# A fourth seven-product chunk pair in every second gate-and-up block of a two-FFN decoder layer

## The chip, the cores and the metric

The kernel runs on one NeuronCore of a Trainium2 chip. The metric is the device time of one execution in microseconds, as the median over several executions. The profiled execution is one more execution of the same program; its span is what the trace covers.

## The reference

The reference is one decoder layer over 256 tokens of width 2048, in float32. Four parts follow each other:

```python
x = x + 0.5 * swiglu(rms_norm(x, ffn1_norm), ffn1_w_gate, ffn1_w_up, ffn1_w_down)
x = gated_parallel_mixer(x, ...)      # sliding-window attention and RWKV-7, gated
x = memory_cross_attention(x, mem, ...)
x = x + 0.5 * swiglu(rms_norm(x, ffn2_norm), ffn2_w_gate, ffn2_w_up, ffn2_w_down)
return rms_norm(x, final_norm)

def swiglu(h, w_gate, w_up, w_down):
    return (silu(h @ w_gate) * (h @ w_up)) @ w_down
```

The hidden width of each feed-forward network is 5632. Only the two feed-forward networks and the place where the mixer's constants are made are touched by the change.

## The kernel before, in words

**Products.** TensorE multiplies in a reduced float32 format, so each operand is split into a high part (a cast on ScalarE, `hi`) and the rest (a subtraction on VectorE, `lo`). One product of a 128x128 block of the activations with a 128x512 piece of weights is three matmuls, L422 (high by high), L423 (high by the weights' low part) and L424 (low by high), in the function `times`. Weights come from memory as float32 (`raw`, `raw2`), are split by `split_raw` (L330 cast, L331 subtraction), and are used by both halves of 128 tokens.

**Blocks.** A feed-forward network has 11 blocks of 512 hidden columns, in groups of 4, 4 and 3 (`GROUPS`). Block 0 multiplies gate and up one after the other (`product`). In blocks 1 to 10 `gate_up` does both in one `product_pair`. Its contraction over 2048 runs in eight chunk pairs q = 0 to 7 of 256 each. After each group come the down products for that group (`down`, also through `product_pair`, or `product`).

**Seven products for eight.** A plain chunk pair takes two halves of tokens times gate and up times two chunks, that is eight products or 24 matmuls. In the chunk pairs of `SEVEN = (0, 2, 4)` a Strassen-like scheme takes seven products, named p1 to p7, or 21 matmuls. It needs four sums of weight pieces t1 to t4, built by `sums` for each chunk pair: L350, L351 and L352 on VectorE, then the cast L355 on ScalarE and the subtraction L356 on VectorE (tiles `thi` and `tlo`, one buffer each). It also needs sums of the activations, built once for each network by `combinations` (L454 to L470; tiles `chi`, `clo`). A plain chunk pair that comes before the last seven-product one (`EARLY`, here 1 and 3) needs another, smaller sum of the activations for p3. Products are added over all eight chunk pairs in PSUM. After the last seven-product pair, `end` (L559 to L561) adds the shared terms, and after q = 7 `finish` (L565 to L577) makes silu(gate) times up.

**Buffers.** `raw2` has 3 buffers, each holding one chunk pair of gate and up. The weights' `hi` and `lo` have 3 buffers each; a seven-product pair fills two of them (`u1g1`, 1024 columns, and `g0`, 512 columns) beside `thi` and `tlo`, and a plain pair fills two of 1024 columns. PSUM has four single banks (`acc`) and two double banks (`two`); p6 and p7 share one double bank, p5 and p3 the other, and the transposes of the block's result (`feats`) use the same two.

**Order.** The program is traced in Python. `next_item` asks for the splits of the present and of the next chunk pair (`AHEAD`), and `Interleave.tick` puts steps of background work between the products: the transposes, the combinations, the norms. A scheduler of the language then fixes the order of each engine's instructions when the program is built, and may place an instruction that its model finds ready ahead of earlier ones. At run time each engine goes through its own fixed list.

**Constants.** Masks and small matrices for the mixer are made at the program's start on GpSimd (L213 to L244) in a pool that lives through the whole kernel.

Of the kernel before, what the change touches and what calls it, by code (L numbers as in the profile page):

```python
# [15 lines left out]
P = 128  # L16
# [24 lines left out]
EARLY = tuple(q for q in range(max(SEVEN)) if q not in SEVEN)  # L41

SEVEN_DOWN = (2, 4)
# [46 lines left out]
def feed_forward_plan(wg, wu, wd):  # L90
    for gi, (j0, nj) in enumerate(GROUPS):
        for j in range(j0, j0 + nj):
            if j == 0:
                for w in (wg, wu):
                    yield w, 0, KD, j * 512, 512
            else:
                yield (wg, wu), 0, KD, (j * 512, j * 512), SEVEN
        for n in (0, 2):
            if n in down_pairs(gi):
                yield (wd, wd), 4 * j0, 4 * nj, (n * 512, n * 512 + 512), SEVEN_DOWN  # L100
            else:
                for m in (n, n + 1):
                    yield wd, 4 * j0, 4 * nj, m * 512, 512
# [37 lines left out]
def decoder_layer(ctx: ExitStack, tc: tile.TileContext, a: dict, out: bass.AP):  # L141
# [71 lines left out]
    identr = cpool.tile([P, P], F32R, name="identr")  # L213
    select(identr[:], ones[:], [[-1, P]], ALU.is_equal, 0.0, 0, 1)
    abias = cpool.tile([P, 2, P], F32R, name="abias")
    pool.memset(f32(abias[:]), 0.0)
    select(abias[:, 0, :], abias[:, 0, :], [[1, P]], ALU.is_gt, NEG, 0, -1)
    select(abias[:, 1, :], abias[:, 1, :], [[-1, P]], ALU.is_ge, NEG, 0, 1)

    ups = cpool.tile([P, P], F32, name="ups")  # L220
    pool.memset(ups[:], UP)
    mask3 = cpool.tile([P, 3, P], F32, name="mask3")
    select(mask3[:, 0, :], ups[:], [[1, P]], ALU.is_gt, 0.0, 0, -1)
    select(mask3[:, 1, :], ups[:], [[1, P]], ALU.is_ge, 0.0, 0, -1)
    select(mask3[:, 2, :], ups[:], [[1, P]], ALU.is_ge, 0.0, 0, -1)

    mask_l = cpool.tile([P, P], F32, name="mask_l")
    select(mask_l[:], ups[:], [[-1, P]], ALU.is_gt, 0.0, 0, 1)
    bdones = cpool.tile([P, P], F32, name="bdones")
    bdmean = cpool.tile([P, P], F32, name="bdmean")  # L230
    bdup = cpool.tile([P, P], F32, name="bdup")
    pool.memset(bdones[:], 0.0)
    pool.memset(bdmean[:], 0.0)
    pool.memset(bdup[:], 0.0)
    for e in range(2):
        q = slice(64 * e, 64 * e + 64)
        pool.memset(bdones[q, q], 1.0)
        pool.memset(bdmean[q, q], 1.0 / 64)
        pool.memset(bdup[q, q], UP)
    center = cpool.tile([P, P], F32, name="center")  # L240
    dve.tensor_tensor(center[:], ident[:], bdmean[:], ALU.subtract)
    keep = cpool.tile([P, 2, P], F32, name="keep")
    pool.memset(keep[:], 1.0)
    pool.memset(keep[:, :, 0:1], 0.0)  # L244
# [189 lines left out]
    def combinations(sp, x, seven, early, ready, tag, apart):  # L434


        n = 4 * len(seven) + 2 * len(early)
        parts = [sp.tile([P, n, P], F32R, tag=tag + e, name=tag + e) for e in ("hi", "lo")]
        c = {"parts": parts, "at": {}, "next": []}

        def work():
            o = 0
            while not ready():
                yield
            yield from idle(apart)
            for q in sorted(seven + early):
                while not all(KU * q + i in x.done for i in range(KU)):
                    yield
                v = sp.tile([P, 2, 2, P], F32, tag="u", name="u", bufs=2)
                f = sp.tile([P, 4, P], F32, tag="u", name="u", bufs=2)  # L450
                n = 4 if q in seven else 2
                s = slice(o, o + n)
                with behind_weights():
                    dve.tensor_tensor(  # L454
                        v[:].rearrange("p k t n -> p k (t n)"), f32(x.at(0, 2 * q, 2)),
                        f32(x.at(1, 2 * q, 2)), ALU.add,
                    )
                    if q in seven:
                        dve.tensor_tensor(f[:, 0], v[:, 0, 1], v[:, 1, 1], ALU.add)
                        dve.tensor_tensor(f[:, 1], f[:, 0], v[:, 0, 0], ALU.subtract)  # L460
                        dve.tensor_tensor(f[:, 2], v[:, 0, 0], v[:, 0, 1], ALU.subtract)
                        dve.tensor_tensor(f[:, 3], v[:, 1, 0], f[:, 1], ALU.subtract)
                    else:
                        dve.tensor_tensor(f[:, :2], v[:, :, 0], v[:, :, 1], ALU.subtract)
                yield from idle(2)
                with behind_weights():
                    act.copy(parts[0][:, s], f[:, :n])
                yield from idle(2)
                with behind_weights():
                    dve.tensor_tensor(  # L470
                        parts[1][:, s], f[:, :n], f32(parts[0][:, s]), ALU.subtract
                    )
                c["at"][q] = o
                o += n
                yield

        bg.spawn("mem", work())
        return c

    def product_pair(x: Act, c, w, four, seven, early, after, end, finish, first=()):  # L480
# [10 lines left out]
        def bank(to):  # L491
            if to in b:
                return
            for pair in PAIRS:
                if to in pair:
                    banks = two()
                    b.update((e, banks[:, i]) for i, e in enumerate(pair))
                    return
            b[to] = acc()
# [12 lines left out]
        def of_c(q, i):  # L512
            return [p[:, c["at"][q] + i, :] for p in c["parts"]]

        p5 = "p8" if four else "p5"
        for q in range(late + 1):
# [3 lines left out]
            if q in seven:  # L520
# [16 lines left out]
                continue  # L537
            u = next_item()
            for i in range(KU):
                for to, t, j in (("p2", 0, 0), ("p4", 1, 0), ("p3", 0, 1), (p5, 1, 1)):  # L540
                    off = to == "p3" and q in early
                    ends = last and i == KU - 1
                    add(to, of_c(q, i) if off else of_x(t, k + i), u[i][j], ends)
# [5 lines left out]
    PAIRS = ("p6", "p7"), ("p5", "p3")  # L549

    def gate_up(sp, x, c, r, w):
        hb = sp.tile([P, 2, 512], F32, tag="hb", name="hb", bufs=2)
        u2, u3 = (sp.tile([P, 512], F32, tag="u", name="u", bufs=2) for _ in range(2))
# [4 lines left out]
        def end(b):  # L558
            dve.tensor_tensor(u2[:], b["p6"], hb[:, 0], ALU.add)  # L559
            dve.tensor_tensor(u3[:], b["p7"], u2[:], ALU.add)  # L560
            dve.tensor_tensor(u2[:], b["p5"], u2[:], ALU.add)  # L561
            while c["next"]:
                bg.spawn("feat", c["next"].pop())

        def finish(to, b):  # L565
# [3 lines left out]
            elif to == "p4":  # L569
                dve.tensor_tensor(hb[:, 1], b["p4"], u3[:], ALU.add)  # L570
                act.activation(hb[:, 1], hb[:, 1], AF.Silu, scale=r[1])
            else:
                t, v = (0, u2) if to == "p3" else (1, u3)
                dve.tensor_tensor(v[:], b[to], v[:], ALU.add)  # L574
                dve.scalar_tensor_tensor(
                    hb[:, t], v[:], r[t], hb[:, t], ALU.mult, ALU.mult
                )  # L577

        product_pair(x, c, w, False, SEVEN, EARLY, after, end, finish)
        return hb  # L580

    def down(sp, h, c, w, xs, then):
# [17 lines left out]

        def residual():
# [3 lines left out]
            for t, v in enumerate((hb, u)):  # L605
                yield
                o = xs(t, 0, 2)
                dve.tensor_tensor(o, v[:].rearrange("p a n -> p (a n)"), o, ALU.add)
# [10 lines left out]
        product_pair(  # L619
            h, c, w, True, SEVEN_DOWN, (), after, end, finish,  # L620
            ("p1", "p5"),
        )
# [99 lines left out]
    def feed_forward(sp, x, norm: Norm, wg, wu, wd, done, begin_last=lambda: None, last=False):  # L722
# [7 lines left out]
        c = combinations(sp, norm.x, SEVEN, EARLY, lambda: norm.r is not None, "c", 4)  # L730
        for gi, (j0, nj) in enumerate(GROUPS):
# [9 lines left out]
            for j in range(j0, j0 + nj):  # L741
                if j > 0:
                    hb = gate_up(sp, norm.x, c, norm.r, wg)
# [11 lines left out]
                for t in range(2):  # L755
                    dve.scalar_tensor_tensor(
                        hb[:, t, :], pu[t], norm.r[t], hb[:, t, :], ALU.mult, ALU.mult
                    )
# [4 lines left out]
            d = combinations(sp, h, SEVEN_DOWN, (), lambda: True, "d", 0)  # L763
            for n in (0, 2):
                if n in down_pairs(gi):
                    down(
                        sp, h, d, wd,
# [4 lines left out]
                for m in (n, n + 1):  # L772
# [3 lines left out]
                    for t in range(2):  # L776
                        xs = x[:, t, m * 512 : (m + 1) * 512]
                        dve.scalar_tensor_tensor(xs, pd[t], 0.5, xs, ALU.mult, ALU.add)
# [70 lines left out]
    with tc.tile_pool(name="mx", bufs=1, reuse_waits="tile") as sp:  # L849
        aligned(sp)  # L850

# [885 lines left out]
```

## Time and profile before

| | |
|---|---|
| median of 3 executions | 2235.72 us (2234.56 to 2239.03) |
| profiled execution | 2236.75 us, span 2235.0 us |
| granted TensorE clock in the profile | 0.999 |
| TensorE matmul busy | 2216.0 us, 99% of the span, 10792 matmuls |
| VectorE busy | 1745.4 us, 78%, 2039 instructions |
| ScalarE busy | 1193.5 us, 53% |
| DMA | 435.40 MB, mean 195 GB/s |

A row of the timeline has the start in us from the span's start, the duration, the engine, the line of the kernel, the operation, output and inputs, their shapes, how many instructions were merged into the row, and in brackets how long the engine was idle before and which instruction ended that. Matmuls overlap, so the time that one costs is the distance between two starts and not its duration. VectorE's instructions overlap a little as well, so the distance of starts is used for them too.

Block j = 1 of the first network runs from about 55 to 97 us, block 2 to about 141 us, block 3 to about 184 us; then follow the down products of the first group. The mixer begins at about 720 us, the second network's block 0 at about 1524 us.

### The profile page before, as it was taken

To read this page: it belongs to the slowest core of one execution; us is meant where nothing else is said; L and a number is where in the kernel's file an instruction comes from. 1 tells how busy PE (TensorE), PEld (TensorE's weight loads), DVE (VectorE), ACT (ScalarE), POOL (GpSimd) and SP (SyncE) were. 2 spreads that over 40 slices of the span, in tenths; PEclk is the share of its full clock that TensorE was granted. 3 is DMA by queue.
4 is the path that set the end of the run, shared out by engine and by line. 5 is a ranking of instruction groups with operands and counts; after the bars stand their busy time and mean duration, and the time that the engine had idled before them with its cause. 6 is when DMAs were issued, how large, how long until landed. Compare 5 with 4: busy or idle time off the path is not lost.

```text
span 2235.0 us, 28341 instructions
## 1 busy us (share of the span) xinstructions
PE 2216.0 (99%) x10792; PEld 1819.2 (81%) x10792; DVE 1745.4 (78%) x2039; ACT 1193.5 (53%) x1434; POOL 81.3 (4%) x151
## 2 busy tenths in 40 slices
PE   9999999999999999999999999999999999999998
PEld 7888888888888877788888878888888888888886
DVE  7988988898987567886465466558888888898887
ACT  6555555555555567444443445556555555555554
POOL 1000000000000000103200100001000000000000
PEclk9999999999999999999999999999999999999999
DMA  7666665566556545677435775547665656566664
GB/s 247 211 220 195 203 207 190 187 208 202 194 193 214 165 130 151 219 219 233 121 102 148 230 266 189 181 164 255 201 207 177 218 193 199 193 202 194 207 203 155
DMA packets 219832, 435.40 MB, mean 195 GB/s; under 512 B 13888, under 2 KB 16016, under 8 KB 219696
## 3 DMA queue, kind: packets, MB, share of 16 engines
q1 hardware_dynamic: 210768, 406.37, 56.8%
q0 software_dynamic: 8352, 26.44, 3.8%
q8 instruction: 84, 1.38, 0.3%
q10 hardware_dynamic: 576, 0.79, 0.1%
q14 instruction: 52, 0.43, 0.1%
HBM read 420.05 MB, written 13.50 MB: 194 GB/s over the span
## 4 chain that ended last, share of the span: by engine, by line
PE 93%; DVE 3%; DMA 2%; ACT 1%; issue 1%; SPq 0%; POOLq 0%; POOL 0%; DVEq 0%; ACTq 0%
PE acc L422 20%; PE acc L423 20%; PE acc L424 20%; PE two L422 9%; PE two L423 9%; PE two L424 9%; PE two L185 2%; DVE lo L331 1%; PE two L177 1%; DMA raw<-in_ffn_w_up_dram 1%; DMA raw<-in_w_proj_rwkv_dram 1%; ACT hi L330 0%; PE two L1279 0%; DMA raw<-in_ffn_w_gate_dram 0%; PE acc L1416 0%
## 5 line engine op out<-in xcount | busy, mean ns | idle before, releaser
L330 ACT CAST hi<-raw 128x1024 fp32r<-128x1024 f32 (+1 forms) x770 | 764.2, 1001 | 783.7 <-PE acc L424 362.1
L331 DVE TENSOR_TENSOR lo<-raw,hi 128x1024 fp32r<-128x1024 f32 (+1 forms) x770 | 882.5, 1156 | 343.0 <-ACT hi L330 342.2
L422 PE MATMUL acc<-hi,xhi 128*128 128x512 f32 (+1 forms) x1256 | 491.2, 392 | 1.9 <-ACT hi L330 1.8
L423 PE MATMUL acc<-lo,xhi 128*128 128x512 f32 (+1 forms) x1256 | 488.2, 389 | 2.8 <-DVE lo L331 2.8
L424 PE MATMUL acc<-hi,xlo 128*128 128x512 f32 (+1 forms) x1256 | 486.9, 388 | 0.0
L422 PEld LDWEIGHTS acc<-hi,xhi 128*128 128x128 f32 x1256 | 235.7, 188 | 56.0 <-issue 5.4
L423 PEld LDWEIGHTS acc<-lo,xhi 128*128 128x128 f32 x1256 | 235.9, 188 | 55.2 <-DVE lo L331 6.7
L424 PEld LDWEIGHTS acc<-hi,xlo 128*128 128x128 f32 x1256 | 235.8, 188 | 47.4 <-DVE xlo L680 0.2
L356 DVE TENSOR_TENSOR tlo<-raw,thi 128x1024 fp32r<-128x1024 f32 x160 | 192.8, 1218 | 0.0
L355 ACT CAST thi<-raw 128x1024 fp32r<-128x1024 f32 x160 | 165.7, 1050 | 36.6 <-DVE raw L350 20.1
L423 PE MATMUL acc<-lo,hhi 128*128 128x512 f32 x424 | 166.4, 392 | 0.0
L424 PE MATMUL acc<-hi,hlo 128*128 128x512 f32 x424 | 165.2, 390 | 0.0
L422 PE MATMUL acc<-hi,hhi 128*128 128x512 f32 x424 | 159.8, 391 | 0.0
L422 PE MATMUL two<-hi,xhi 128*128 128x512 f32 x320 | 125.7, 393 | 0.0
L424 PE MATMUL two<-hi,xlo 128*128 128x512 f32 x320 | 124.6, 389 | 0.0
L423 PE MATMUL two<-lo,xhi 128*128 128x512 f32 x320 | 124.6, 389 | 0.0
L350 DVE TENSOR_TENSOR raw<-raw 128x1024 f32<-128x1024 f32 x80 | 97.5, 1219 | 15.4 <-DMA raw<-in_ffn_w_up_dram 13.1
L423 PEld LDWEIGHTS acc<-lo,hhi 128*128 128x128 f32 x424 | 79.6, 188 | 19.4 <-DVE lo L331 3.1
L422 PEld LDWEIGHTS acc<-hi,hhi 128*128 128x128 f32 x424 | 79.1, 188 | 18.6 <-ACT hi L330 2.6
L424 PEld LDWEIGHTS acc<-hi,hlo 128*128 128x128 f32 x424 | 79.6, 188 | 16.2
L422 PEld LDWEIGHTS two<-hi,xhi 128*128 128x128 f32 x320 | 60.1, 188 | 13.4 <-DVE u L574 0.2
L424 PEld LDWEIGHTS two<-hi,xlo 128*128 128x128 f32 x320 | 60.1, 188 | 12.6
(374 smaller groups left out, 3186.2 us busy)
## 6 DMA issues: line engine op xcount, KB each, us to landing
raw<-in_ffn_w_gate_dram SPq DMA_DIRECT2D x167, 512.0 KB, 3.8
raw<-in_ffn_w_up_dram SPq DMA_DIRECT2D x160, 512.0 KB, 4.7
raw<-in_ffn_w_down_dram SPq DMA_DIRECT2D x152, 512.0 KB, 4.8
raw<-in_w_in_dram SPq DMA_DIRECT2D x136, 512.0 KB, 3.7
raw<-in_w_out_dram SPq DMA_DIRECT2D x32, 512.0 KB, 3.6
raw<-in_ffn_w_down_dram SPq DMA_DIRECT2D x12, 1024.0 KB, 5.2
raw<-in_ffn_w_up_dram SPq DMA_DIRECT2D x8, 1024.0 KB, 7.9
raw<-in_w_proj_attn_dram SPq DMA_DIRECT2D x16, 512.0 KB, 4.2
```

The lines of the kernel that those rows point to most:

```text
L177: prev = pe.matmul(to, lhs, rhs, **how)
L185: prev = pe.transpose(to, src, ident[:])
L330: newest["act"] = act.copy(hi[:, s], raw[:, s])
L331: newest["dve"] = dve.tensor_tensor(lo[:, s], raw[:, s], f32(hi[:, s]), ALU.subtract)
L350: dve.tensor_tensor(ta[:], raw[:, 1:3], raw[:, 0:2], ALU.subtract)
L355: act.copy(hi[:, s], t[:])
L356: dve.tensor_tensor(lo[:, s], t[:], f32(hi[:, s]), ALU.subtract)
L422: pe.matmul(o, xh, hi, start=first, stop=False, **how)
L423: pe.matmul(o, xh, lo, start=False, stop=False, **how)
L424: newest["pe"] = pe.matmul(o, xl, hi, start=False, stop=last, **how)
```

## The change

- In odd blocks (1, 3, 5, 7, 9 of each network) `gate_up` takes seven products in chunk pairs 0, 2, 3 and 4 (`MORE`); even blocks keep 0, 2 and 4. Chunk pairs 2, 3 and 4 of an odd block are then three seven-product pairs in a row, and the weight plan follows.
- `combinations` builds the activation sums for 0, 2, 3 and 4, and the smaller ones for 1 and 3, so that chunk pair 3 has both kinds (6 sets where there were 5). Its work tile becomes one buffer of [128, 2, 512] in place of two of 512 columns.
- The last steps of both token halves become one: p3 and p5 are added to their shared terms in one instruction of 1024 columns after p5, and multiplied with the silu in a second one. The norm's factor is no longer multiplied in here.
- That factor, times 0.5, is applied where the down products are added to the residual stream. Block 0 and `down` change with it.
- The mixer's constants are made at the start of the mixer, in its own pool, in place of the program's start.

```diff
+MORE = (0, 2, 3, 4)
 SEVEN_DOWN = (2, 4)
+def early(*sets):
+    return tuple(sorted({q for s in sets for q in range(max(s)) if q not in s}))
+def seven_up(j):
+    return MORE if j % 2 else SEVEN
...
-                yield (wg, wu), 0, KD, (j * 512, j * 512), SEVEN
+                yield (wg, wu), 0, KD, (j * 512, j * 512), seven_up(j)
...
-    identr = cpool.tile([P, P], F32R, name="identr")
...
+    def mixer_constants(sp):
+        identr = sp.tile([P, P], F32R, name="identr")
...
-            for q in sorted(seven + early):
+            for q in sorted(set(seven + minus)):
...
-                v = sp.tile([P, 2, 2, P], F32, tag="u", name="u", bufs=2)
-                f = sp.tile([P, 4, P], F32, tag="u", name="u", bufs=2)
+                w = sp.tile([P, 2, 512], F32, tag="u", name="u", bufs=1)
...
+                todo = []
+                if q in seven:
+                    todo.append(4)
+                if q in minus:
+                    todo.append(2)
...
-    PAIRS = ("p6", "p7"), ("p5", "p3")
+    PAIRS = ("p6", "p7"), ("p3", "p5")
...
-            else:
-                t, v = (0, u2) if to == "p3" else (1, u3)
-                dve.tensor_tensor(v[:], b[to], v[:], ALU.add)
-                dve.scalar_tensor_tensor(
-                    hb[:, t], v[:], r[t], hb[:, t], ALU.mult, ALU.mult
-                )
-
-        product_pair(x, c, w, False, SEVEN, EARLY, after, end, finish)
+            elif to == "p5":
+                dve.tensor_tensor(u[:], b["p3", "p5"][:], u[:], ALU.add)
+                dve.tensor_tensor(hb[:], u[:], hb[:], ALU.mult)
+
+        product_pair(x, c, w, False, seven, early(seven), after, end, finish)
...
-        def half(o, of, in1):
-            dve.scalar_tensor_tensor(o, of, 0.5, in1, ALU.mult, ALU.add)
-
         def after(b):
-            act.activation(hb[:, 0], b["p1"], AF.Copy, scale=0.5)
+            act.copy(hb[:, 0], b["p1"])
 
         def end(b):
-            half(hb[:, 1], b["p6"], hb[:, 0])
-            half(u[:, 0], b["p7"], hb[:, 1])
-            half(hb[:, 1], b["p5"], hb[:, 1])
-            half(u[:, 1], b["p5"], u[:, 0])
+            dve.tensor_tensor(hb[:, 1], b["p6"], hb[:, 0], ALU.add)
+            dve.tensor_tensor(u[:, 0], b["p7"], hb[:, 1], ALU.add)
+            dve.tensor_tensor(hb[:, 1], b["p5"], hb[:, 1], ALU.add)
+            dve.tensor_tensor(u[:, 1], b["p5"], u[:, 0], ALU.add)
...
+        def scaled_onto(t, o, v):
+            dve.scalar_tensor_tensor(o, v, r[t], o, ALU.mult, ALU.add)
...
-                dve.tensor_tensor(o, v[:].rearrange("p a n -> p (a n)"), o, ALU.add)
+                scaled_onto(t, xs(t, 0, 2), v[:].rearrange("p a n -> p (a n)"))
...
-            half(xs(t, n, 1), b[to], xs(t, n, 1))
+            scaled_onto(t, xs(t, n, 1), b[to])
...
-        c = combinations(sp, norm.x, SEVEN, EARLY, lambda: norm.r is not None, "c", 4)
+        c = combinations(
+            sp, norm.x, MORE, early(SEVEN, MORE), lambda: norm.r is not None, "c", 4
+        )
+        half = stat.tile([P, 2], F32, tag="half", name="half", bufs=2)
...
-                    dve.scalar_tensor_tensor(
-                        hb[:, t, :], pu[t], norm.r[t], hb[:, t, :], ALU.mult, ALU.mult
-                    )
+                    dve.tensor_tensor(hb[:, t, :], pu[t], hb[:, t, :], ALU.mult)
+                    dve.tensor_scalar(half[:, t : t + 1], norm.r[t], 0.5, None, ALU.mult)
...
+            r = [half[:, t : t + 1] for t in range(2)]
...
-                        dve.scalar_tensor_tensor(xs, pd[t], 0.5, xs, ALU.mult, ALU.add)
+                        dve.scalar_tensor_tensor(xs, pd[t], r[t], xs, ALU.mult, ALU.add)
...
     with tc.tile_pool(name="mx", bufs=1, reuse_waits="tile") as sp:
         aligned(sp)
+        mixer_constants(sp)
```

More of the change, by code (lines that the diff above doesn't have):

```diff
@@ L232, in decoder_layer @@
[L232 to L244, printed above, removed]
+    c_ = {}
@@ L432, in multiply, with combinations @@
             )
-    def combinations(sp, x, seven, early, ready, tag, apart):
-        n = 4 * len(seven) + 2 * len(early)
+    def combinations(sp, x, seven, minus, ready, tag, apart):
+        n = 4 * len(seven) + 2 * len(minus)
         parts = [sp.tile([P, n, P], F32R, tag=tag + e, name=tag + e) for e in ("hi", "lo")]
-        c = {"parts": parts, "at": {}, "next": []}
+        c = {"parts": parts, "at": {}, "minus": {}, "next": []}
         def work():
@@ L477, in combinations, with product_pair @@
         bg.spawn("mem", work())
         return c
-    def product_pair(x: Act, c, w, four, seven, early, after, end, finish, first=()):
+    def product_pair(x: Act, c, w, four, seven, minus, after, end, finish, first=()):
         pw, _, nk, _, n = plan[at["product"]]
@@ L850, in decoder_layer @@
         aligned(sp)
+        mixer_constants(sp)
+        identr, abias, mask3, mask_l, bdones, bdmean, bdup, center, keep = (
+            c_[n] for n in (
+                "identr", "abias", "mask3", "mask_l", "bdones", "bdmean", "bdup", "center",
+                "keep",
+            )
+        )
         def t4(name, shape=(P, 4, T), dt=F32):
```

130 lines of the change are left out of this document (74 added, 56 removed).

## The prediction

> **What bounds the kernel now.** I read the page first, for the engines' shares and the chain of waits.
>
> ```profile
> span 2235.0 us, 28341 instructions
> PE 2216.0 (99%) x10792; PEld 1819.2 (81%) x10792; DVE 1745.4 (78%) x2039; ACT 1193.5 (53%) x1434; POOL 81.3 (4%) x151
> PE 93%; DVE 3%; DMA 2%; ACT 1%; issue 1%; SPq 0%; POOLq 0%; POOL 0%; DVEq 0%; ACTq 0%
> ```
>
> TensorE sets the end: 93% of the chain is matmuls. So a matmul less is a gain, as long as its operands come in time. VectorE's 78% is a mean over unlike stages, so I asked next for busy time by stretch: first the start of block 1 of the first network, then block 3 up to its last seven-product pair, then the rest of block 3.
>
> ```profile
> 55.00:81.00 26.00, 26.00 (x118) 20.91 (x118) 25.92 (x34) 16.04 (x19) 0.00 (x0) 1.00 0.57 184
> 139.00:160.70 21.70, 21.70 (x96) 17.68 (x95) 21.32 (x25) 12.59 (x14) 0.00 (x0) 1.00 0.66 220
> 160.70:181.00 20.30, 20.30 (x95) 16.89 (x95) 11.60 (x11) 9.35 (x10) 0.00 (x0) 1.00 0.61 186
> ```
>
> The third busy time is VectorE's: 25.92 of 26.00 us, 21.32 of 21.70, then 11.60 of 20.30. In the first half of a block VectorE is full and just keeps up; in the second it rests. The change adds work exactly to the full half. So I looked at block 3, an odd one, on both engines: VectorE up to the end of its preparations for q = 4, and TensorE during q = 4.
>
> ```profile
> 142.44 0.75 DVE L575 SCALAR_TENSOR_TENSOR hb<-u,rs,hb 128x512 f32<-128x512 f32 x1
> 143.10 0.68 DVE L574 TENSOR_TENSOR u<-two,u 128x512 f32<-128x512 f32 x1
> 143.70 1.22 DVE L331 TENSOR_TENSOR lo<-raw,hi 128x1024 fp32r<-128x1024 f32 x1
> ...
> 151.85 1.22 DVE L350 TENSOR_TENSOR raw<-raw 128x1024 f32<-128x1024 f32 x1
> 152.98 2.35 DVE L331 TENSOR_TENSOR lo<-raw,hi 128x1024 fp32r<-128x1024 f32 x2
> 155.25 0.68 DVE L351 TENSOR_TENSOR raw<-raw,raw 128x512 f32<-128x512 f32 x1
> 155.97 0.69 DVE L352 TENSOR_TENSOR raw<-raw,raw 128x512 f32<-128x512 f32 x1
> 156.58 1.22 DVE L331 TENSOR_TENSOR lo<-raw,hi 128x1024 fp32r<-128x1024 f32 x1
> 157.71 2.35 DVE L356 TENSOR_TENSOR tlo<-raw,thi 128x1024 fp32r<-128x1024 f32 x2
> 159.98 0.68 DVE L331 TENSOR_TENSOR lo<-raw,hi 128x512 fp32r<-128x512 f32 x1
> ```
>
> ```profile
> 160.98 0.39 PE L422 MATMUL acc<-hi,xhi 128*128 128x512 f32 x1
> 161.20 0.39 PE L423 MATMUL acc<-lo,xhi 128*128 128x512 f32 x1
> ...
> 163.24 0.39 PE L423 MATMUL two<-tlo,chi 128*128 128x512 f32 x1
> ...
> 165.28 0.39 PE L423 MATMUL two<-tlo,chi 128*128 128x512 f32 x1
> 165.74 0.39 PE L422 MATMUL acc<-hi,xhi 128*128 128x512 f32 x1
> ```
>
> TensorE runs without a gap: 21 matmuls of q = 4 from 160.98 to 165.74, 0.2267 us each. VectorE has the parts of q = 4 ready at 160.06 (`tlo`) and 160.66 (`g0`), hardly before they are used.
>
> **1. Matmuls removed.** A plain pair has 24, a seven-product pair 21. Five odd blocks in two networks: 10 x 3 = 30 matmuls, 30 x 0.2267 = **6.80 us** (0.68 a block). That is the whole gain that TensorE can give. [...]
>
> **2. VectorE work added to an odd block.** By the distances of starts in block 3's rows a seven-product pair costs 1.13 (L350) + 0.72 + 0.61 (L351, L352) + 2.27 (L356, two) + 1.13 (L331, 1024 columns) + about 0.6 (L331, 512 columns) = 6.5 us; a plain pair costs two L331, 2.27. The fourth one adds 4.2. The merged last step takes off a little: L574 (0.60) and L575 (0.66) twice are 2.52, two instructions of 1024 columns at 1.13 are 2.26, so -0.26. TensorE comes 0.68 earlier at the end of q = 3. So at q = 4 VectorE is late by 4.2 - 0.26 + 0.68 = **4.6 us** more than today.
>
> **3. How much lateness q = 4 bears.** The last `tlo` is ready at 160.06. In today's order it is needed at 163.24 (p6), 3.2 us later; if p5 to p7 and p4 are put last in q = 4, not before about 165.28, 5.2 us later. So with a good order 5.2 - 4.6 = 0.6 us are left and nothing stalls. That the list of TensorE is rewritten so where VectorE is late is seen in block 1, where q = 4 runs from about 76.5 to 81.4:
>
> ```profile
> 77.71 1.22 DVE L356 TENSOR_TENSOR tlo<-raw,thi 128x1024 fp32r<-128x1024 f32 x1
> ```
>
> ```profile
> 77.14 0.39 PE L423 MATMUL two<-tlo,chi 128*128 128x512 f32 x1
> 77.37 0.39 PE L423 MATMUL acc<-lo,xhi 128*128 128x512 f32 x1
> ...
> 78.42 0.40 PE L424 MATMUL two<-thi,clo 128*128 128x512 f32 x1
> 78.89 0.39 PE L422 MATMUL acc<-thi,xhi 128*128 128x512 f32 x1
> ...
> 80.96 0.39 PE L423 MATMUL two<-tlo,chi 128*128 128x512 f32 x1
> ```
>
> There the three matmuls of one product are torn apart, p1 and p2 come between those of p7, and the start distances stay at 0.23. What is left over in q = 5 to 7 is 8.7 us of rest (20.30 - 11.60), so a late block does not pass its lateness on. I take a stall of 0.15 us in each of nine odd blocks, **+1.3 us**: near 0, which the 0.6 would give, as block 1's starts keep their distance though VectorE is full there; the other end is 1.4 each, 4.6 less the 3.2 of today's order.
>
> **4. The new wait: `thi` and `tlo` have one buffer.** Today a plain pair lies between two seven-product pairs; now the casts for q = 3 and 4 can begin only after the last product that reads the old ones. On ScalarE they queue ahead of the `hi` casts, on VectorE the two L356 wait behind them.
>
> ```profile
> 156.01 2.00 ACT L355 CAST thi<-raw 128x1024 fp32r<-128x1024 f32 x2
> ```
>
> The first cast is half of these 2.00, the first L356 1.13, the second 1.22 until it is done, and I allow 0.1 for each of two handings over: the last `tlo` is ready 3.6 us after the pair before has ended. With the products that need it put last it is needed 4.3 us into the pair (165.28 - 160.98): hidden, 0.7 us to spare, so 0. In today's order of p6 it is needed after 2.3 us (163.24 - 160.98): 1.3 us. That is the same order and the same stall as in step 3, not a second one.
>
> **5. Block 1 of the first network.** Here the combinations still run, and VectorE has no rest from 55 to 81.
>
> ```profile
> 70.08 0.28 DVE L461 TENSOR_TENSOR u<-u 128x128 f32<-128x128 f32 x1
> 70.28 0.28 DVE L460 TENSOR_TENSOR u<-u 128x128 f32<-128x128 f32 x1
> 72.95 0.68 DVE L470 TENSOR_TENSOR clo<-u,chi 128x512 fp32r<-128x512 f32 x1
> ```
>
> The second set for q = 3 adds four small ones, 0.20 apart, and one like L470, 0.6 by the distance of 512-column starts: 1.4 us. With 4.2 and 0.68 that makes 6.3 us. The last `tlo` was ready at 77.71 + 1.22 = 78.93 and used last at 80.96: 2.0 us to bear. Stall 6.3 - 2.0 = **+4.3 us**, once. The ends are 6.3, if nothing is borne, and 4.3 - 3.6 = 0.7, if work moves ahead into the rest that VectorE had earlier:
>
> ```profile
> 35.36 1.23 DVE L331 TENSOR_TENSOR lo<-raw,hi 128x1024 fp32r<-128x1024 f32 x1 [3.56 <-ACT hi L330]
> ```
>
> I take 4.3, as the combinations are put into the list by steps between products and come no earlier. In the second network the norm is known before block 0, so they are nearly done by block 1; I count it among the nine.
>
> **6. The rest.** The factor in `down` costs 0.06 us an instruction (L575 0.75 against L574 0.68), 0.1 us of it at the very end. The constants leave the start, where nobody waits for them, for the mixer's: GpSimd must wait there until the stream x has been stored, and one VectorE subtraction (`center`) and all splits behind it wait for GpSimd.
>
> ```profile
> 719.30 0.73 POOL L840 DMA_DIRECT2D x1d<-x  x1 [16.02 <-DVE x L778]
> 727.86 0.73 POOL L718 TENSOR_TENSOR rs<-ms,nhalf 128x2 f32<-128x2 f32 x1 [6.82 <-DVE ms L716]
> ```
>
> The gap of 6.8 us between these two holds the constants; the norm's factor behind them is first read after a whole product. I take 0, between 0 and 3 us. SP's queue and the bytes loaded stay as they are.
>
> **Sum.** -6.80 + 1.3 + 4.3 + 0.1 = -1.1 us. The profiled execution took 2236.75 us, so 2235.65; it lies 1.03 us above the median of the runs, which I put at 2235.72 - 1.1 = **2234.6 us**.
>
> **Rivals.** A: *nearly all of it is hidden, block 1 too* (0.7 us there, nothing elsewhere): -6.8 + 0.7 + 0.1 = -6.0, 2229.7. For it speaks VectorE's rest of 3.56 us, against it the full 25.92. B (slower): *TensorE's list keeps its order in q = 3 and 4, and p6 waits in each odd block.* Its price is 1.4 us by step 3, 9 x 1.4 = 12.6, so -6.8 + 12.6 + 4.3 + 0.1 = +10.2, 2245.9. If p1 too stays first, it bears only 161.20 - 160.66 = 0.5, where 160.66 is the last L331's start and duration, and the price is 4.1 a block, some 2270. B decides from 0.8 us a block on, which makes +4.8. For it: no two seven-product pairs follow each other today, so no row shows such a list; against it, the torn products of block 1. [...] C: *the mixer's start loses 3 us*: 2237.6, still no change.
>
> **Chances.** 0.2% of this kernel, 4.5 us, is about what a measurement can tell from no change. Forecast and C, within it: 0.44. A, and a small stall in block 1: faster 0.27. B, from 0.8 us a block on: slower 0.29. The range of 8 in 10 runs from A, 2229, to a little over B, 2247; the forecast's own is 2231 to 2239.
>
> **What would show it.** Right: 10762 matmuls; odd blocks 0.68 us shorter than even ones with the same transposes; L356 three times running with a pair's length between; products torn in q = 3 and 4 with starts 0.23 apart; a gap of some 4 us between 65 and 82 us put down to L356 or L331. Wrong: waits for L356 or L331 of a microsecond in every odd block; none in block 1; a hole near 725 us.

## The result, and the profile after

The changed kernel takes 2268.51 us (median of 4 runs, 2268.02 to 2270.62), the kernel before 2236.51 us beside it: ratio 1.0144, 95% interval 1.0127 to 1.0162. It is 32 us slower; I had forecast 2234.6 and a range up to 2247.

The page of the changed kernel: the span, the engines' busy time, and the chain of waits by engine.

```profile
span 2266.4 us, 28362 instructions
PE 2242.5 (99%) x10762; PEld 1810.1 (80%) x10762; DVE 1787.5 (79%) x2063; ACT 1201.8 (53%) x1456; POOL 79.8 (4%) x151
PE 90%; DVE 5%; DMA 2%; ACT 1%; issue 1%; SPq 0%; POOL 0%; POOLq 0%; DVEq 0%; ACTq 0%
```

The 30 matmuls are gone (10792 to 10762), and yet TensorE's busy time grew by 26.5 us. So most of the loss does not look like waiting. The view of TensorE's waits (waited for, us in total, times, longest) holds few us:

```profile
PE acc L437 <- DVE lo L345: 7.0, 9, 2.0
PE acc L436 <- ACT hi L344: 2.0, 2, 1.2
...
PE two L437 <- DVE lo L345: 1.7, 2, 0.8
```

Of before, the same view has nearly as much:

```profile
PE acc L423 <- DVE lo L331: 4.7, 8, 1.1
...
PE acc L422 <- ACT hi L330: 1.8, 2, 1.2
```

Next I compared stretches that hold the same work, by busy time: from the copy of p1 in `down` to the first silu of the next block, which has `down`'s second pair of columns and most of a block with three seven-product pairs. First before, then after; the columns are PE, PEld, DVE, ACT and POOL, the granted clock, and DMA.

```profile
249.84:309.79 59.95, 59.95 (x266) 49.52 (x265) 53.57 (x59) 29.93 (x33) 0.00 (x0) 1.00 0.62 204
```

```profile
259.15:320.07 60.92, 60.92 (x266) 49.73 (x265) 54.07 (x59) 29.94 (x33) 0.00 (x0) 1.00 0.61 199
```

The same 266 matmuls, TensorE busy without a gap in both, the clock at 1.00 in both: 0.97 us more. Only the distance of the starts shows why. Here are the first and the last row of the longest unbroken run of products that read `hhi` and `hlo` (TensorE's timeline, start and duration), before and after:

```profile
210.97 0.39 PE L422 MATMUL acc<-hi,hhi 128*128 128x512 f32 x1
...
238.62 0.39 PE L424 MATMUL acc<-hi,hlo 128*128 128x512 f32 x1
```

```profile
218.56 0.39 PE L436 MATMUL acc<-hi,hhi 128*128 128x512 f32 x1
...
247.72 0.40 PE L438 MATMUL acc<-hi,hlo 128*128 128x512 f32 x1
```

Before, the 122 distances between these starts make 27.65 us, 0.2266 us each; after, 125 make 29.16, **0.2333 us each**. Sorted by the stationary tile (the second name behind the arrow; the first is the streamed one), over the whole trace: products of `hi`, `lo` with `hhi`, `hlo` went from 227.6 to 233.8 ns, with the combinations from 226.8 to 233.4, with the mixer's tiles from 227.6 to 233.7, with the features `xhi`, `xlo` only from 227.2 to 228.2. Some 3200 products with 6 ns more, and 860 of `thi`, `tlo` with 4 ns more, are about 23 us, and some 4400 products of the features with 1 ns more another 4. (These means, and those of the table below, are of distances up to about 0.3 us; with other ways to count near that limit they move by some 0.4 ns, nearly alike in all runs.)

Second, block 1 of the first network. Stretches of 2 us, after, the clock behind POOL's busy time:

```profile
76.00:78.00 2.00, 1.45 (x7) 0.86 (x5) 2.00 (x3) 0.46 (x1) 0.00 (x0) 1.00 1.02 395
78.00:80.00 2.00, 0.96 (x3) 0.48 (x3) 2.00 (x3) 0.58 (x1) 0.00 (x0) 1.00 0.03 12
80.00:82.00 2.00, 0.44 (x1) 0.44 (x2) 2.00 (x4) 1.04 (x1) 0.00 (x0) 0.90 0.00 0
82.00:84.00 2.00, 1.91 (x5) 1.00 (x5) 2.00 (x6) 1.14 (x2) 0.00 (x0) 0.50 0.62 131
84.00:86.00 2.00, 1.91 (x7) 1.00 (x6) 2.00 (x3) 1.01 (x2) 0.00 (x0) 0.75 0.98 380
86.00:88.00 2.00, 2.00 (x11) 1.62 (x10) 0.93 (x2) 0.00 (x0) 0.00 (x0) 1.00 0.25 47
```

VectorE is full (2.00 of 2.00) and TensorE starves; and behind the holes the clock is granted at half (0.50) for 3.4 us. The timeline has the waits, both put down to the split of the weights, and then rows of 0.63 us in place of 0.39:

```profile
78.62 0.50 PE L437 MATMUL acc<-lo,xhi 128*128 128x512 f32 x1 [1.17 <-DVE lo L345]
...
81.56 0.79 PE L437 MATMUL acc<-lo,xhi 128*128 128x512 f32 x1 [1.98 <-DVE lo L345]
82.15 0.63 PE L438 MATMUL acc<-hi,xlo 128*128 128x512 f32 x1
82.58 0.63 PE L436 MATMUL acc<-thi,xhi 128*128 128x512 f32 x1
```

By the first silu of block 1 the changed kernel is 7.5 us behind (104.88 against 97.36).

### The profile page after: what moved, and what is told of

It is laid out like the page before. It is cut to its first block, busy times and chain, and to the rows that moved or that the text cites. A ratio compares the mean times of both kernels' runs of the same rounds, so it can differ in the third digit from the quotient of the medians.

```text
span 2266.4 us, 28362 instructions
## 1 busy us (share of the span) xinstructions
PE 2242.5 (99%) x10762; PEld 1810.1 (80%) x10762; DVE 1787.5 (79%) x2063; ACT 1201.8 (53%) x1456; POOL 79.8 (4%) x151
## 4 chain that ended last, share of the span: by engine, by line
PE 90%; DVE 5%; DMA 2%; ACT 1%; issue 1%; SPq 0%; POOL 0%; POOLq 0%; DVEq 0%; ACTq 0%
PE acc L436 19%; PE acc L437 19%; PE acc L438 19%; PE two L437 9%; PE two L438 8%; PE two L436 8%; PE two L192 2%; DVE lo L345 2%; PE two L184 1%; DMA raw<-in_w_proj_rwkv_dram 1%; DMA raw<-in_ffn_w_up_dram 1%; ACT hi L344 0%; PE two L1306 0%; DMA raw<-in_ffn_w_gate_dram 0%; DVE tlo L370 0%
## 5 line engine op out<-in xcount | busy, mean ns | idle before, releaser
L344 ACT CAST hi<-raw 128x1024 fp32r<-128x1024 f32 (+1 forms) x770 | 756.5, 993 | 756.3 <-PE acc L438 401.9
L436 PE MATMUL acc<-hi,xhi 128*128 128x512 f32 (+1 forms) x1236 | 483.7, 394 | 2.1 <-ACT hi L344 2.0
L369 ACT CAST thi<-raw 128x1024 fp32r<-128x1024 f32 x180 | 185.7, 1047 | 63.9 <-DVE raw L364 21.9
L370 DVE TENSOR_TENSOR tlo<-raw,thi 128x1024 fp32r<-128x1024 f32 x180 | 216.8, 1218 | 0.0
L364 DVE TENSOR_TENSOR raw<-raw 128x1024 f32<-128x1024 f32 x90 | 109.6, 1218 | 13.8 <-DMA raw<-in_ffn_w_up_dram 12.2
L436 PE MATMUL two<-hi,xhi 128*128 128x512 f32 x300 | 118.1, 394 | 0.0
L437 PE MATMUL two<-lo,xhi 128*128 128x512 f32 x300 | 117.2, 391 | 0.0
L438 PE MATMUL two<-hi,xlo 128*128 128x512 f32 x300 | 117.1, 390 | 0.0
L437 PEld LDWEIGHTS acc<-lo,hhi 128*128 128x128 f32 x424 | 79.5, 188 | 20.7 <-DVE lo L345 1.2
L438 PE MATMUL two<-thi,clo 128*128 128x512 f32 x210 | 82.8, 394 | 0.0
L437 PE MATMUL two<-tlo,chi 128*128 128x512 f32 x210 | 82.5, 393 | 0.0
```

The lines of the kernel that those rows point to most:

```text
L344: newest["act"] = act.copy(hi[:, s], raw[:, s])
L364: dve.tensor_tensor(ta[:], raw[:, 1:3], raw[:, 0:2], ALU.subtract)
L369: act.copy(hi[:, s], t[:])
L370: dve.tensor_tensor(lo[:, s], t[:], f32(hi[:, s]), ALU.subtract)
L436: pe.matmul(o, xh, hi, start=first, stop=False, **how)
L437: pe.matmul(o, xh, lo, start=False, stop=False, **how)
```

## The experiments

**Where tiles stand.** What could slow products with `h` but hardly with the features? Both networks' pools, and the mixer's, lie behind the pool of small statistics, and the change puts a new tile there, `half`: two buffers, 32 bytes of each partition apiece. By the addresses that the build assigns, all of the streamed weights (`hi`, `lo`), the features and the blocks' tiles were at remainder 224 by 256 before; after, weights and features still are, and everything behind `half` is at 32. The first four runs undid the shift, made it alone, moved everything, and took the fourth pair out.

```diff
 e1_place          (changed)  half = stat.tile([P, 2], ..., bufs=2)  ->  bufs=4
 e2_place_before   (before)  +stat.tile([P, 2], F32, tag="pad", name="pad", bufs=2)   # 64 bytes
 e3_start0_before  (before)  +cpool.tile([P, 8], F32, name="pad")                      # 32 bytes, ahead of all
 e4_no_fourth      (e1)       seven_up(j): return SEVEN
```

> The changed kernel with the small tile half in four buffers instead of two: the tiles behind it (blocks' sums, h, combinations, mixer) move 64 bytes up in each partition, back to the same remainder by 128 (96) as before the change; no instruction is added or taken. Theory P (place: products whose stationary side lies at remainder 32 come every 0.2333 us instead of 0.2267, some 3900 of them): 2268.5 - 25 = about 2243, and no tile's mean spacing above 0.229. Theory V (the fourth seven-product pair: waits for VectorE and a slower TensorE beside it): 2268 as the changed kernel, since nothing of its work or order moves.

> The kernel before with an unused pad of 64 bytes in the pool of small statistics, nothing else. Theory P: the stationary tiles behind it go to remainder 32 by 128, some 3700 products 0.0065 us slower: 2236.5 + 24 = about 2260. Theory V: 2236.5, no change.

> The kernel before with an unused pad of 32 bytes in the pool of constants: all tiles, the weights' and the features' too, start at remainder 0 by 128 instead of 96. Theory P has two forms. P-same (what counts is that the two operands of a product lie at the same remainder): 2236.5, no change. P-start (each remainder has its own price): another time than 2236.5, faster if a start at a whole line is the best one, slower if remainder 96 was. Theory V: 2236.5.

> As e1 (place restored), with the fourth seven-product pair undone: odd blocks take three as before; the merged last step, the factor in down's sum, the moved constants and the larger table of combinations stay. Theory P with my prediction's price of the pair (waits of about 1 us per odd block, 5 to 6 us in the first block, against 6.8 us saved): about 2238, near the kernel before, and 5 below e1. Theory V: the whole loss is the pair's, so 2237 here and 2268 in e1.

Measured, with 2236.49 for before: e1 2269.68, e2 **2261.12** (ratio 1.011, 1.0095 to 1.0125), e3 2235.72 (0.9996, 0.9986 to 1.0005), e4 2265.75. An unused pad of 64 bytes costs the kernel before 24.6 us, with no other edit. Its stretch like those above, and its waits:

```profile
253.12:314.03 60.91, 60.91 (x266) 49.73 (x265) 53.67 (x59) 29.94 (x33) 0.00 (x0) 1.00 0.61 200
```

```profile
PE acc L423 <- DVE lo L331: 3.7, 7, 1.0
PE acc L422 <- ACT hi L330: 2.6, 2, 1.4
```

60.91 us for the same 266 matmuls, as in the changed kernel; the waits (6.3 us) are less than before's (6.5). So place is a cause by itself, and no row of waits shows it. But e1 and e4 missed: remainder 96 by 128, as before, did not bring the rate back (products with `h` at 232.9 ns). In e1 the tiles stand 128 behind the weights by 256. So the period is longer than 128, or it is not a matter of distance. And e3 moved all tiles alike and changed nothing.

**Distance or place, and the period.** "Same remainder as the weights by 1024" needs 960 more bytes in the changed kernel, "by 256 alone" 192.

```diff
 e5_pad960            (changed) +stat.tile([P, 240], F32, tag="pad", name="pad", bufs=1)
 e6_all_by_64         (before)  +cpool.tile([P, 16], F32, name="pad")     # ahead of all
 e7_pad192            (changed) +stat.tile([P, 48], F32, tag="pad", name="pad", bufs=1)
 e8_pad960_no_fourth  (e5)       seven_up(j): return SEVEN
```

> The changed kernel with an unused pad of 960 bytes behind the tile half, so that the stationary tiles and the streamed ones (hi, lo) have the same remainder by 1024 again, as before the change (992 and 992). Theory R (the distance between the two operands' places counts, and 1024 is enough): the 25 us of the slow products go, 2268.5 - 25 = about 2244. Theory A (the remainder 224 by 256 of each tile counts by itself): 2244 too. Theory V (the fourth pair makes the rate drop, by whatever it does beside TensorE): 2268.

> The kernel before with an unused pad of 64 bytes ahead of all tiles that the products read: every tile is at remainder 32 by 256, the one of the slow tiles in the 64-byte run, but the distances between them are those of before. Theory R: 2236.5, no change. Theory A: all products are slow now, at least the 24.6 us of the 64-byte run, so 2261, and up to 10700 x 0.0062 = 66 us if the features' products follow: 2261 to 2302.

> The changed kernel with an unused pad of 192 bytes behind half: stationary and streamed tiles have the same remainder by 256 (224), but not by 512 or 1024. Theory R with a period of 256, and theory A: 2244 as with 960. Theory R with a longer period (512 or 1024): about 2268, the products stay at 0.233 us.

> The 960-byte pad on the changed kernel without its fourth seven-product pair (odd blocks take three as before; merged last step, factor, moved constants and the larger table stay). From the two 128-byte runs the pair costs 2269.7 - 2265.8 = 3.9: so 2244 - 4 = about 2240 if place and pair add up, and what is left above 2236.5 is the rest of the change (some 4). If the pair's price hung on the slow rate, it comes out with its own sign here: 2251 (the 6.8 us that it saves) if it has no waits of its own.

Measured, with 2237.41 for before: e5 2253.40, e7 2254.03, e6 2236.19 (0.9995, 0.9986 to 1.0005), e8 2245.03. Theory A falls with e6: at remainder 32, the one of the slow tiles, everything runs at 227 ns so long as all stand there. e5 and e7 agree: a period of 256 is enough. All products of e5 are back at 227 to 229 ns. It gains 15.1 us rather than 25, and e8 on e4 gains 20.7. The rest went into waits and dips of the clock: distances of starts above 0.3 us, less 0.227 each, sum to 43.8 us in the changed kernel's trace and to 54.9 in e5's, the half clock in block 1 lasted 3.4 and 6.8 us, and the mean granted clock was 0.998 and 0.996. So the pair now costs 8.4 us (e5 less e8) where it cost 3.9 at the slow rate (e1 less e4).

**The price by distance.** One more pad (e9) moved the weights and all else off the features instead. Then four pads of other sizes stood where e2 had its 64 bytes.

```diff
 e9_weights_from_x  (before) +wp.tile([P, 16], F32, tag="pad", name="pad", bufs=1)   # features stay, all else +64
 p1 .. p4           (before) +stat.tile([P, n], F32, tag="pad", name="pad", bufs=1)  # 32, 128, 192, 256 bytes
```

> The kernel before with an unused pad of 64 bytes between the features (xhi, xlo) and everything behind them: the streamed tiles and the blocks' own stationary tiles keep their distance of 0 by 256, and the features are now 64 off the weights that stream over them. Theory R (a product is slow when its stationary and its streamed tile lie at different remainders by 256): the 4700 products of the features come every 0.2335 us, the others every 0.227: 2237 + 4700 x 0.0062 = 2266. Theory X (only tiles that other engines write in the same blocks pay, as h and the combinations are): the features are written once, so 2237 to 2240.

> The kernel before with an unused pad of 32 bytes at the same place as the pad of 64 that cost 24.6 us. If the price comes from any distance that is not a multiple of 256, some 3700 products at 5 to 6.5 ns: 2255 to 2261. If 64 is the smallest step that counts: 2237.

> The same with 128 bytes. By the changed kernel with that distance (stationary tiles of the blocks at 232.9 ns, 5.5 more than at distance 0): 2237.2 + 3700 x 0.0055 = 2258. If the work of the changed kernel was the cause there: 2237.

> The same with 192 bytes: the stationary tiles stand 192 after the streamed ones by 256, as the features did in the run that put them 64 before. Theory R (the distance sets the price): 2.1 ns a product as measured there, 2237.2 + 3700 x 0.0021 = 2245. Theory K (the kind of tile sets it: h, the combinations and the mixer's tiles are slow wherever they stand off, the features hardly): as with 64, 2257 to 2261.

> The same with 256 bytes, the control: with a period of 256 the price is nothing, 2237. A longer period (512, 1024), which the two padded forms of the changed kernel already speak against, would leave 2257 to 2261.

| stationary tile stands after the streamed one by (modulo 256) | `hi`, `lo` with `hhi`, `hlo`: mean distance of starts, ns | time, us |
|---|---|---|
| 0 (before) | 227.6 | 2237.1 |
| 32 (p1) | 233.8 | 2259.8 |
| 64 (e2) | 233.8 | 2261.1 |
| 128 (p2) | 233.0 | 2259.2 |
| 192 (p3) | 230.8 | 2250.5 |
| 256 (p4) | 227.6 | 2236.1 |
| 192, the features only (e9) | 229.3 (`xhi`, `xlo`) | 2244.5 |

The e9 run fell between its two theories (2266, and 2237 to 2240): the features' products got slower by 2.1 ns and not by 6. First and last row of 122 distances in p3 (0.2289 us each in this run of rows) and in p4 (0.2267):

```profile
211.29 0.40 PE L422 MATMUL acc<-hi,hhi 128*128 128x512 f32 x1
...
239.22 0.39 PE L424 MATMUL acc<-hi,hlo 128*128 128x512 f32 x1
```

```profile
210.50 0.39 PE L422 MATMUL acc<-hi,hhi 128*128 128x512 f32 x1
...
238.16 0.39 PE L424 MATMUL acc<-hi,hlo 128*128 128x512 f32 x1
```

The control confirms the period (p4: 0.9999, 0.9989 to 1.0008). At 192 the price is about half for `h` (3.2 of 6.2 ns) and a third for the features (2.1): the distance sets most of it, not the kind of tile, though my 2245 for p3 was 5 us too low. The kept traces show the same the other way round: where `thi`, `tlo` stream over the features, the stationary tile stands 192 after the streamed one in e2 and 64 after it in p3, and the products come every 229.0 and 234.0 ns (227.0 before). One row of the account does not fit: in e2, `thi` and `tlo` stand at distance 0 from the combinations, all 64 off the rest, and their products still came every 230.3 ns. So the distance between a product's own two operands does not set all of it; what else does was not tried. Why the rate, 227.6 to 233.8 ns in the table, goes with the place of the operands, the runs do not show.

**What the pair costs, and where.** With places right (e5's pad), three kernels took the fourth pair out of block 1, spread it, or left only the rest of the change.

```diff
 e11_no_block1          (e5) return MORE if j % 2 and j > 1 else SEVEN
 e10_spread_from_block2 (e11) MORE = (0, 2, 4, 6); combinations for q = 5, 6 made after block 1
 e12_rest_only          (e8) combinations(sp, norm.x, SEVEN, early(SEVEN), ...)
```

> The changed kernel with the 960-byte pad, the fourth pair at q=6 instead of q=3 (0, 2, 4, 6: a plain pair after each), only from block 2 of each network on, and the combinations for pairs 5 and 6 made after block 1. Theory L (VectorE is late by some tenths where two seven-product pairs follow each other, 0.7 us of short waits an odd block, and late by microseconds in the first block, where it also makes the combinations): block 1 is back to the 2.3 to 4.8 us of the runs without a fourth pair or below, and the eight odd blocks keep their 0.68 us each: 2245.0 - 5 - 5.4 = about 2235 if the smaller table ahead of block 1 brings that block back to before, 2239 if not. Rival S (the single buffers of thi and tlo or the whole load of VectorE set the waits, wherever the pair stands): odd blocks as with q=3, so 2241 to 2245.

> The changed kernel with the 960-byte pad, its fourth pair left out of block 1 of each network, eight odd blocks keep it. If block 1 of the first network carries most of what the pair costs (3.3 us of 8.4 by the marks of the two traces, and the halved clock there), 2253.4 - 3.3 = 2250 at most; with odd blocks that only break even (0.7 saved, 0.7 waited) 2245 to 2247. If every odd block loses by a microsecond as in my rival B, 2245.0 + 8 x 1.4 = 2256 would need the block 1 of the changed kernel to cost nothing.

> The changed kernel with the 960-byte pad, three seven-product pairs everywhere and the table of combinations of before (its third pair's four columns not made): what is left of the change is the merged last step, the norm's factor in down's sum and the moved constants. My prediction prices these at 0.1 + 0 to 3: 2237 to 2240. If the 4.8 us at the first network's start in the run with the larger table come from the merged step or the factor, they stay: 2243 to 2245.

Measured, with 2237.18 for before: e11 2247.75, e10 2243.34, e12 2243.04. So block 1 of the two networks carries 5.65 of the pair's 8.4 us (e5 less e11), the other eight odd blocks 2.7 (e11 less e8), and the larger table 2.0 (e8 less e12). In eight blocks 24 matmuls are saved, 5.4 us, so 5.4 + 2.7 = 8.1 us are waited: **1.0 us an odd block**. It is not one wait. Block 3 of the second network, from silu to silu, before and in e5:

```profile
1651.23:1693.04 41.81, 41.81 (x190) 34.63 (x190) 32.83 (x36) 22.43 (x25) 0.00 (x0) 1.00 0.63 201
```

```profile
1665.63:1707.48 41.85, 41.85 (x187) 33.61 (x186) 36.43 (x39) 23.49 (x26) 0.00 (x0) 1.00 0.62 198
```

187 matmuls take as long as 190 did. In e5's timeline the products of this block's q = 4 are torn apart, each one a tenth or two late:

```profile
1688.35 0.68 PE L436 MATMUL two<-thi,chi 128*128 128x512 f32 x2
1688.87 0.40 PE L437 MATMUL acc<-lo,xhi 128*128 128x512 f32 x1
1689.26 0.50 PE L436 MATMUL acc<-thi,xhi 128*128 128x512 f32 x1
1689.59 0.40 PE L438 MATMUL acc<-hi,xlo 128*128 128x512 f32 x1
1689.88 0.51 PE L437 MATMUL two<-tlo,chi 128*128 128x512 f32 x1
```

From 1688.87 to 1690.22, the next start, there are four distances in 1.35 us, 0.34 each instead of 0.227. Such holes sum to 0.7 us in this block against 0.08 before, and the block behind it waits too, as this row of e11 shows:

```profile
1882.74 0.50 PE L437 MATMUL acc<-lo,xhi 128*128 128x512 f32 x1 [0.16 <-DVE lo L345]
```

Most of the rows torn here read `thi` and `tlo`, which have one buffer each. ScalarE could cast the new `thi` only when TensorE had done with the pair before:

```profile
1687.19 2.01 ACT L369 CAST thi<-raw 128x1024 fp32r<-128x1024 f32 x2 [2.17 <-PE acc L438]
```

Such a wait of 2.1 to 2.4 us stands in nine of e5's ten odd blocks and in all eight of e11's that have the fourth pair, and nowhere in before or e8. VectorE has no rest there either (in the block shown its rows lie end to end from 1683.40 to 1692.10), so the runs do not part the two.

e10 tells against my theory L: with a plain pair behind each seven-product pair the time is that of the rest alone (2243.3 against 2243.0). So what the eight pairs save is waited again, or goes into the combinations for q = 5 and 6, which e12 does not make; e10 does not part these. One wait there stands at q = 7, on the sums that VectorE forms after the last seven-product pair:

```profile
1865.43 0.50 PE L436 MATMUL two<-hi,xhi 128*128 128x512 f32 x1 [0.27 <-DVE u L587]
```

**The rest of the change.** e12 has no fourth pair and no larger table, and is still 5.9 us over before (1.0025, 1.0015 to 1.0035). Two runs undid one part each.

```diff
 r1_rest_unmerged   (e12) p3 and p5 added and multiplied by themselves again, as soon as each ends
 r2_rest_constants  (e12) mixer_constants(cpool) at the start instead of mixer_constants(sp) at the mixer
```

> The run of the rest alone (2243.0), with the last step of each half by itself again, without its scalar. If the merged step makes the waits (the pair's two sums stay in their bank until one addition at the end has read both): some 2 to 3 us go, 2240 to 2241, and the wait of 0.5 us ahead of block 3 is gone. If it does not: 2243.

> The run of the rest alone (2243.0), with the mixer's constants made at the start as before. If the move costs at the mixer's start what the marks show there (0.8 us) and makes the dip of the clock at 22 to 25 us more likely (1.3 us): 2241 to 2242. My prediction's price for the move is 0 to 3. If it costs nothing: 2243.

Measured, with 2236.87 for before: 2242.24 (1.0023, 1.0014 to 1.0031) and 2242.27 (1.0023, 1.0014 to 1.0032). Neither moves the time by more than the runs scatter, so neither carries the 5.9 us. What both and e12 share, and before has not, is a wait at the end of each network, where VectorE adds the factored sums; in e12:

```profile
687.75 1.29 DVE L620 SCALAR_TENSOR_TENSOR x<-hb,half,x 128x1024 f32<-128x1024 f32 x1
688.95 1.22 DVE L345 TENSOR_TENSOR lo<-raw,hi 128x1024 fp32r<-128x1024 f32 x1
```

```profile
690.22 0.50 PE L437 MATMUL two<-lo,hhi 128*128 128x512 f32 x1 [0.93 <-DVE lo L345]
```

The holes there are 1.1 us and come in both networks: 2.2 of the 5.9. By the starts in e12's trace the others are small: 1.5 for a dip of the clock at 22 to 26 us (below), about 0.9 ahead of and in block 3 (among it 0.48 on `u` L597, the merged step's own wait, which is gone in r1), 0.4 to 0.6 in each of four groups' `down`, 0.5 at 1538 us; the mixer gives 1.0 back, with one wait of 1 us for `lo` around 1305 us where before has two. r1, which loses nothing up to block 3, has four of these waits in the mixer and so ends at the same time. Which edit brings the waits in `down` and at the networks' ends was not tried by itself: the factor and the new order of VectorE's list came in one.

## Why the prediction was wrong, by its steps

**Step 1** held for the count (10762 matmuls) and, without saying so, priced all the others at 0.2267 us still. That is the step that failed first, a term put at nothing without a reason: products whose stationary tile lies behind the new tile `half` came every 0.233 us. The change's own 64 bytes are worth 24.6 us in the kernel before (e2) and 15.1 in the changed one (e5), where waits filled part of what was given back. The trace of before held no sign of it, as all tiles stood at one remainder; the line that adds `half` is in the diff, and **step 6** looked only at the instructions that read it.

**Step 2** held about: in the block of the second network shown above VectorE's busy time grew from 32.83 to 36.43, by 3.6 us, for 4.2 less 0.26 forecast.

**Step 3** put a stall of 0.15 us into an odd block, with ends 0 and 1.4. The runs give 1.0. The torn products of q = 4 came as described, but "nothing stalls" was wrong twice: torn products pay a tenth or two each, and the lateness does reach the next block. So the 0.68 us that an odd block saves is spent.

**Step 4** priced the single buffers of `thi` and `tlo` at nothing. Their wait came in nearly each odd block, and the times it gave fit: in the block shown above the last `tlo` is ready at 1690.96 (the view of VectorE: 1688.61, two L370 in 2.35), 3.8 us after the pair before has ended, for 3.6 forecast. What failed is "hidden": the products of q = 4 that read these tiles are the ones that pay the tenths. How much of the 1.0 us is this wait's and how much VectorE's lateness stays open. e10 frees the tiles early and is 4.4 us faster than e11, but it also makes a part of the combinations later, and it has its own wait on the sums.

**Step 5** (block 1, +4.3 with the new combinations) had the place and the cause right, and the size wrong. e5 less e11 is 5.65 us although 1.4 of matmuls are saved in two blocks, so some 7.0 us of waits, and the larger table adds 2.0: 9.0 in place of 4.3. (By the starts of the first silu in the traces, the first network's block 1 alone has 7.1 of this: e5 is 6.4 us behind e12 there, with 0.7 saved.) What I left out is the clock. In e5 the starts from 85.34 to 89.18 us lie 0.43 apart, nearly twice 0.2267, and the half clock began at 82.3: about 3 us more, behind 4 us of holes. The step also read one row wrongly. The `tlo` used at 80.96 is a part that was ready early; by the addresses of the build, the part ready at 78.93 is first read at 79.11. In that order 0.2 us were to bear and not 2.0, and the 165.28 of step 3 has the same slip: both hold only if the list is rewritten.

**Step 6** took 0.1 for the factor and 0, at most 3, for the constants; the rest of the change costs 5.9 us. There was no hole near 725 us, so the constants' gap on GpSimd did hide, and making them at the start again (r2) gains nothing measurable. The largest of the waits, 2.2 us, came where the factor is applied, at the networks' ends, for which the step counted 0.1; whether the factor brought them is open.

The parts against the measured loss: place 15.1 (2268.5 less 2253.4), pair 8.4, table 2.0, rest 5.9, together 31.4 of the 32.0 us. They hold for this order of undoing the parts: alone, in the kernel before, the place costs 24.6.

**Rivals.** A fell. B gave 2246 or, with p1 too at its place, "some 2270", close to the time by luck, as the cause is another: its wait of 1.4 or 4.1 us per odd block is not in the trace, since the list was rewritten and the odd blocks outside the first wait tenths at a time. C's hole at the mixer's start was not seen. None of the three held a slower rate.

## What to carry to other kernels

A new tile moves all that is allocated behind it; here 64 bytes cost 24.6 us (e2). So compare the addresses of stationary and streamed tiles modulo 256 before and after a change, and pad back what moved (192 bytes gave 14.5 us back in e7). When a loss shows in no wait, count matmuls and starts in stretches of equal work. A saving on TensorE that loads an engine already full can come back as waits: here an odd block saved 0.68 us and waited 1.0, by a tenth or two at a time. And holes close to each other can go with a loss of the clock as well: here two of 1.3 and 2.2 us, then 3.4 us at half clock.

## What the runs showed of the hardware that I had not expected

- In these runs the rate of 128x512 products went, for the most part, with the distance between stationary and streamed tile in the partition, modulo 256 bytes: `hi`, `lo` with `hhi`, `hlo` came every 227.6 ns at 0, 233.8 at 32 and 64, 233.0 at 128, 230.8 at 192; the exception is the 230.3 ns at distance 0 in e2. Moving all tiles alike changed nothing (e3 0.9996, e6 0.9995).
- In block 1 of the changed kernel two holes of 1.3 and 2.2 us (distance of starts less a matmul's 0.23: 77.05 to 78.62, 79.18 to 81.56) were followed by a granted clock of 0.50 for 3.4 us.
- The clock's records of two traces read so. Before: from 6.8 us on full for 2222.08 us, then half up to the end. Changed kernel: from 6.5 us on full for 75.09 us, half for 3.41, full for 2177.70, then half up to the end. The four lengths are 651, 22, 1 and 638 times 3.413 us. In e5 the half clock from 82.3 to 89.2 us lasted two such lengths, in e12 that from 22.4 to 25.8 one. Counted by such lengths from the first full grant on, the one just ahead of the half clock in the changed kernel, 78.18 to 81.60 us, has 2.69 us of holes (distances above 0.3 us, less 0.227). No other at full clock has more than 1.40 there, and none more than 1.48 before. Before has two holes at 18 to 22 us (1.35 and 1.00 us) that fall into two such lengths, parted at 20.4 us, and no half clock follows. That the sum of holes within one length decides is my estimate from these counts; no run was made to try it. In e12 the dip, eight matmuls at nearly double distance, about 1.5 us, reads so (stretches as above):

```profile
22.00:24.00 2.00, 2.00 (x7) 1.53 (x7) 2.00 (x5) 1.60 (x3) 0.00 (x0) 0.59 0.68 198
24.00:26.00 2.00, 2.00 (x7) 1.58 (x6) 1.53 (x3) 0.10 (x1) 0.00 (x0) 0.56 0.82 229
```
